# Routing on un-normalised tokens, a first gather for expert 0, the rest loop ahead of the last expert, and a diagonal norm

## The chip, the core and the metric

The kernel runs on one core of a Trainium2 chip. The metric is the device time of one launch in microseconds; less is better. The core has a matrix engine (TensorE, PE in the profile, with its weight loads as PEld), VectorE (DVE), ScalarE (ACT), GpSimd (POOL) and SyncE (SP), whose queue issues nearly all transfers, and 16 DMA engines which carry them out.

## What is computed

Two transformer blocks on 256 tokens of 1024 features. The part that matters, cut from the reference:

```python
mix = merged @ w_out[l] + b_out[l]
x = layer_norm(DEEPNORM_ALPHA * x + mix, ln1_g[l], ln1_b[l])
ffn = hier_moe(x, ...)      # 8 groups of 8 experts
x = layer_norm(DEEPNORM_ALPHA * x + ffn, ln2_g[l], ln2_b[l])

def hier_moe(...):
    _, g_sel = lax.top_k(g_logits, 1)              # one group of 8
    e_logits = jnp.take_along_axis(e_all, g_sel[:, :, None], axis=1)[:, 0]
    top_v, top_i = lax.top_k(e_logits, TOP_K)      # two experts of its 8
    weights = g_w * jax.nn.softmax(top_v, axis=-1)
    ...                                            # hdn = silu(xb @ w1[e]) * (xb @ w3[e]); hdn @ w2[e]
```

Block 2 begins with an RMS norm (`mix_norm`) ahead of its input projections (a linear recurrence and an attention), has a second one ahead of the FFN and a third ahead of the last gate.

## The kernel before

Tokens lie in two tiles t of 128 (`x1`, 128 partitions x 2 x 1024). A weight of a projection comes as a 1 MB load of 128x2048 floats; ScalarE casts it to a high half (`hlh`, L293), VectorE takes the rest as a low half (`hll`, L295), and three matmuls of the halves make up for one in full precision (L323, L324, L326 with features on partitions; L342, L343, L346 with tokens on partitions). `pump` runs small deferred pieces between the groups of a projection.

**Into the expert loop.** The out-projection (`proj_tok` in `block1`) writes the sum for LN1. `route` then normalises on VectorE (L371, L378), transposes (L785), computes 72 router logits per token (L789, L793), finds the best group and twice the best expert with `first_max` (L814 to L818), and counts with matmuls the rank of each token within its expert (L849 to L853). From the ranks, 0/1 matrices G (L971) are made for four experts at a time, and `gather` multiplies the tokens with G (L885), so that each expert gets 32 slots of features (`xg`). Softmax and slot weights (L857 to L866, L974) lie between these steps.

**The expert loop.** 64 experts of six 1 MB loads each: four for the first stage (L904), two for the halves c=0 and c=1 of the second (L921). Loads go out on SP in the order of the code, each into a buffer of a pool; the list `turn` says which pool comes next (`s1`, `g8`, `ring`, `ring2`, `ring3`, `pa`). A load waits on SP until its buffer's last reader is done, and all loads behind it wait too; eight DMA semaphores used in turn allow eight loads in flight. After a group of four experts `combine` adds its slots to the sums (L933); that of experts 56 to 59 is held back and put between the pieces of expert 63.

**Out of the loop.** 32 slots per expert may be too few; `moe_rest` loops over what is left, under a condition that every engine reads from memory (L1055) and branches on (L1056). For these inputs the loop isn't run. It stands between the two halves of expert 63's second stage. LN2 follows (L360 to L378), then block 2's first norm: squares (L1117), a factor per token (L1126, L1127), the product with the gain (L1132), 16 transposes (L1136) and the split into halves (L300).

**Ahead of the gates.** `ple_norm` does the FFN's norm and the last gate's: first eight matmuls of the gate's own projection (L1169), then the norm of both token tiles.

## Time and profile before

| | before |
|---|---|
| median of 3 runs | 1716.72 us (1716.57 to 1718.79) |
| profiled execution | 1719.65 us, span 1717.8 us |
| TensorE busy | 1486.6 us, 87% of the span |
| VectorE, ScalarE busy | 742.0 us (43%), 512.7 us (30%) |
| transfers | 537.88 MB, 313 GB/s over the span |
| first stages of the experts (L904) | 312.9 us busy, 95.1 us idle before them |

The span falls into three parts: projections of block 1 (to 267 us) with routing behind them, the expert loop (to about 1210 us), and block 2. A window row gives, for a stretch, how long each engine was busy and what the transfers moved; a timeline row gives the start and the length of a run of like instructions, and in brackets how long the engine had been idle and what released it. Matmuls overlap, so the length of a row is a little longer than the time to the next row.

### The profile page before, as it was taken

To read this page: it belongs to the slowest core of one execution; us is meant where nothing else is said; L and a number is where in the kernel's file an instruction comes from. 1 tells how busy PE (TensorE), PEld (TensorE's weight loads), DVE (VectorE), ACT (ScalarE), POOL (GpSimd) and SP (SyncE) were. 2 spreads that over 40 slices of the span, in tenths; PEclk is the share of its full clock that TensorE was granted. 3 is DMA by queue.
4 is the path that set the end of the run, shared out by engine and by line. 5 is a ranking of instruction groups with operands and counts; after the bars stand their busy time and mean duration, and the time that the engine had idled before them with its cause. 6 is when DMAs were issued, how large, how long until landed. Compare 5 with 4: busy or idle time off the path is not lost. (4 is left out here: it accounts for less than half of the span.)

```text
span 1717.8 us, 33678 instructions
## 1 busy us (share of the span) xinstructions
PE 1486.6 (87%) x14724; PEld 1158.9 (67%) x14724; DVE 742.0 (43%) x1464; ACT 512.7 (30%) x911; POOL 17.0 (1%) x22
## 2 busy tenths in 40 slices
PE   8999998867677787878878878767699999999998
PEld 7898996544344455555545545533599998899986
DVE  7999966211111111111111111111676976666645
ACT  4554542111011011011011101111395554555433
POOL 0000000000000000000000000000001000000000
PEclk9999999987777788787688878887899999999999
DMA  7565588999999999999999999999544444545552
GB/s 277 202 208 200 199 338 342 419 419 420 420 421 419 419 420 419 421 419 420 420 420 419 419 421 419 420 398 390 194 154 172 151 170 145 198 180 183 185 190 74
DMA packets 75659, 537.88 MB, mean 313 GB/s; under 512 B 8436, under 2 KB 8564, under 8 KB 11382
## 3 DMA queue, kind: packets, MB, share of 16 engines
q1 hardware_dynamic: 75506, 535.69, 78.2%
q8 instruction: 117, 1.92, 0.4%
q14 instruction: 32, 0.26, 0.0%
q10 hardware_dynamic: 4, 0.01, 0.0%
HBM read 534.62 MB, written 1.05 MB: 312 GB/s over the span
## 5 line engine op out<-in xcount | busy, mean ns | idle before, releaser
L904 PE MATMUL ps<-w,xg 128*32 128x256 f32 x4096 | 312.9, 453 | 95.1 <-DMA w<-in_wm_dram 93.9
L295 DVE TENSOR_TENSOR hll<-w,hlh 128x2048 fp32r<-128x2048 f32 (+1 forms) x114 | 257.1, 2257 | 102.6 <-PE ps L326 54.2
L904 PEld LDWEIGHTS ps<-w,xg 128*32 128x32 f32 x4096 | 135.4, 125 | 245.3 <-DMA w<-in_wm_dram 134.6
L293 ACT CAST hlh<-w 128x2048 fp32r<-128x2048 f32 (+1 forms) x114 | 214.4, 1880 | 171.2 <-PE ps L324 78.7
L323 PE MATMUL ps<-s,hlh 128*128 128x256 f32 x864 | 217.1, 289 | 0.0
L921 PE MATMUL ps<-w,hT 128*32 128x128 f32 x4096 | 177.1, 337 | 45.8 <-DVE hT L915 16.9
L324 PE MATMUL ps<-s,hlh 128*128 128x256 f32 x864 | 212.7, 284 | 0.5 <-DVE s L300 0.5
L910 DVE TENSOR_TENSOR h<-h,ps 64x256 f32<-64x256 f32 x64 | 27.1, 423 | 408.8 <-ACT h L909 408.8
L921 PEld LDWEIGHTS ps<-w,hT 128*32 128x32 f32 x4096 | 145.6, 136 | 65.3 <-issue 28.9
L323 PEld LDWEIGHTS ps<-s,hlh 128*128 128x128 f32 x864 | 165.6, 192 | 3.4 <-issue 2.2
L324 PEld LDWEIGHTS ps<-s,hlh 128*128 128x128 f32 x864 | 165.9, 192 | 1.6 <-DVE s L300 1.2
L909 ACT ACTIVATE h<-ps 64x256 f32<-64x256 f32 x64 | 24.2, 378 | 431.1 <-PE ps L904 431.1
L925 DVE COPY ys<-ps 32x128 f32<-32x128 f32 x240 | 68.2, 284 | 151.6 <-PE ps L921 149.9
L925 ACT COPY ys<-ps 32x128 f32<-32x128 f32 x240 | 62.0, 258 | 230.5 <-PE ps L921 229.1
L326 PE MATMUL ps<-s,hll 128*128 128x256 f32 x864 | 121.4, 283 | 0.0
L326 PEld LDWEIGHTS ps<-s,hll 128*128 128x128 f32 x864 | 111.5, 192 | 0.0
L505 DVE SCALAR_TENSOR_TENSOR w<-w,vec,w 128x255 f32<-128x255 f32 (+14 forms) x240 | 94.3, 465 | 0.0
L323 PE MATMUL ps<-w,hlh 128*128 128x256 f32 x352 | 86.7, 285 | 0.0
L324 PE MATMUL ps<-w,hlh 128*128 128x256 f32 x352 | 85.4, 281 | 0.0
L1109 PEld LDWEIGHTS ps<-rel,con 32*128 32x128 f32 x512 | 78.4, 236 | 10.2 <-issue 7.7
L1109 PE MATMUL ps<-rel,con 32*128 32x8 f32 x512 | 81.8, 290 | 0.0
L913 PEld LDWEIGHTS ps<-con,h 64*128 64x128 f32 x128 | 14.6, 158 | 98.8 <-DVE h L910 98.8
(342 smaller groups left out, 1774.5 us busy)
## 6 DMA issues: line engine op xcount, KB each, us to landing
w<-in_wm_dram SPq DMA_DIRECT2D x384, 1024.0 KB, 19.8
w<-in_w_dram SPq DMA_DIRECT2D x115, 1024.0 KB, 4.9
gain<-in_row_dram SPq DMA_DIRECT2D x4, 512.0 KB, 5.6
w<-in_row_dram SPq DMA_DIRECT2D x3, 512.0 KB
w<-in_wpp_dram SPq DMA_DIRECT2D x2, 768.0 KB
w<-in_xT_dram SPq DMA_DIRECT2D x2, 512.0 KB, 5.4
w<-in_w_dram SPq DMA_DIRECT2D x2, 512.0 KB, 7.3
x<-in_x_dram SPq DMA_DIRECT2D x1, 1024.0 KB, 6.7
```

The costliest lines, as they stand in the source:

```text
L293: nc.scalar.copy(hi[:, ks], src[:, ks])
L295: nc.vector.tensor_tensor(lo[:, ks], src[:, ks], hi[:, ks].bitcast(F32), ALU.subtract)
L323: nc.tensor.matmul(o, hi[:, k, ms], xh[:, k, :], start=(k == 0), stop=False)
L324: nc.tensor.matmul(o, hi[:, k, ms], xl[:, k, :], start=False, stop=False)
L326: nc.tensor.matmul(o, lo[:, k, ms], xh[:, k, :], start=False, stop=(k == 7))
L505: nc.vector.scalar_tensor_tensor(a, u[:, m, :T - d], wj, a, ALU.mult, ALU.add)
L904: r = nc.tensor.matmul(pa[j * 32:(j + 1) * 32, :256], xg[:, k, c0:c0 + CAP], w[:, j * 256:(j + 1) * 256], start=(k == 0), stop=(k == KC - ...
L909: nc.scalar.activation(h, pa[0:64, :256], AF.Silu)
L910: nc.vector.tensor_tensor(h, h, pa[64:128, :256], ALU.mult)
L921: r = nc.tensor.matmul(py[j % 2][j * 32:(j + 1) * 32, :P], hT[:, k % 2, k // 2, :], w[:, j * P:(j + 1) * P], start=(k == 0), stop=(k == 3) ...
L925: eng(ys[r0:r0 + CAP, c * 512 + j * P:c * 512 + (j + 1) * P], py[j % 2][j * 32:(j + 1) * 32, :P])
L1109: nc.tensor.matmul(ps[:, i * 8:(i + 1) * 8], self.con[0:32, o + x:o + x + P], rel, start=True, stop=True)
```

## The change

**Routing.** LN1's row loads and its VectorE passes go. The router weights are multiplied by LN1's gain (`rscale`) and centred over the features (`rcenter`, eight matmuls with ones), so the logits are computed on the un-normalised sum. The first half of its features is transposed and multiplied inside the out-projection (`xT`, `logits`); only the second half stays behind it. LN1 itself is one ScalarE operation per tile, without gain and bias, which the evacuation of the gather applies.

```diff
-            self.fg += [rbias0, nop, rbias1]
+            self.fg += [rbias0, rscale, rbias1, rcenter, nop, lambda: xT(0, 0), lambda: xT(0, 1), lambda: (logits(0, 0), logits(0, 1))]
...
+            for t in range(NT):
+                logits(1, t)
+            for t in range(NT):
+                nc.scalar.activation(x1[:, t, :], x1[:, t, :], AF.Identity, bias=nb[t], scale=rs[t])
```

The order on TensorE shows it at the end of the out-projection. Before (`ps_2592`, `ps_2621` are transposes of the two tiles, `ps_2604` logits):

```order
L346 MATMUL ps_2502<-hll_2536,m_2156 128x512 x4
L785 MATMUL ps_2592<-con,x_71 128x128 x4
L785 MATMUL ps_2598<-con,x_71 128x128 x4
L789 MATMUL ps_2604<-wsm_89,w_2582 128x72 x8
L785 MATMUL ps_2621<-con,x_71 128x128 x4
L785 MATMUL ps_2627<-con,x_71 128x128 x4
L789 MATMUL ps_2633<-wsm_89,w_2582 128x72 x4
```

Here nothing of the routing lies ahead of the last projection matmul. After, from the second of the two groups of transposes that now lie in the projection:

```order
L733 MATMUL ps_2553<-con,x_71 128x128 x4
L360 MATMUL ps_2509<-hlh_2549,m_2156 128x512
L361 MATMUL ps_2509<-hlh_2549,m_2157 128x512
L360 MATMUL ps_2509<-hlh_2549,m_2156 128x512
L361 MATMUL ps_2509<-hlh_2549,m_2157 128x512
L360 MATMUL ps_2509<-hlh_2549,m_2156 128x512
L361 MATMUL ps_2509<-hlh_2549,m_2157 128x512
L360 MATMUL ps_2509<-hlh_2549,m_2156 128x512
L361 MATMUL ps_2509<-hlh_2549,m_2157 128x512
L364 MATMUL ps_2509<-hll_2550,m_2156 128x512 x4
L740 MATMUL ps_2571<-wsm_89,w_2416 128x72 x4
L740 MATMUL ps_2576<-wsm_89,w_2416 128x72 x4
```

Behind this comes the projection's last group of 12 matmuls; the centring (L721, eight matmuls) lies some 60 instructions earlier.

**Top two, ranks, weights.** `nc.vector.max` and `match_replace` take the place of the second and third `first_max`; the ranks come from float32r matmuls on the 0/1 matrices, counted from 1; softmax and slot weights are computed after expert 0's gather.

```diff
-        v1, e1 = first_max(el, "a")
-        nc.vector.scalar_tensor_tensor(el, e1, -3.0e38, el, ALU.mult, ALU.add)
-        v2, e2 = first_max(el, "b")
+        for t in range(NT):
+            nc.vector.max(v8[:, t, :], el[:, t, :])
+        nc.vector.tensor_copy(m8[:, :, 0:2], v8[:, :, 0:2])
+        for t in range(NT):
+            nc.vector.match_replace(ee[:, t, :], m8[:, t, :], el[:, t, :], -3.3e38)
+        nc.vector.tensor_scalar(ee, ee, -3.3e38, None, ALU.is_equal)
...
-        nc.vector.tensor_scalar(rk, rk, -1.0, None, ALU.add)
```

**Gather and residual.** Expert 0's 32 slots are gathered first, between its own first matmuls; the other three experts' 96 slots after expert 0. The residual, formerly four matmuls in the routing (L802), is added at expert 4 from LN1's rows, which take a buffer of `s1` after expert 3.

```diff
+                pre = self.gather(G, xg, 1) if n0 else ()
...
+                    if e == 0:
+                        for f in self.gather(G, xg, 4, 1):
+                            f()
+                        cnt = weights()
+                        slot_weights()
...
+                    if e == 3:
+                        ln1 = self.t(self.s1, [P, 2048], "w")
+                        ln1_rows = self.spread_row(ln1[:, 0:D], "ln1_g") + self.spread_row(ln1[:, D:], "ln1_b")
+                    if e == 4:
+                        for f in ln1_rows + self.residual(ln1):
+                            f()
...
-                + [self.s1] * 2 + [self.ring] * N_RING[0] + [ring3] * N_RING[2]
+                + [self.s1] + [self.ring] * N_RING[0] + [ring3] * N_RING[2] + [self.s1]
```

Experts 60 to 63 get a list of pools of their own (`last`). On SP's queue the loads from the projection's end on stood so (a wait on `PE_49` is one for a TensorE instruction; `w_2958` is the load that waits for the projection's last matmul):

```order
L264 DMA w_2958<-in_wm_dram 128x2048 [waits DMAHW7_49,PE_49]
L264 DMA w_2960<-in_wm_dram 128x2048 [waits DMAHW0_49]
L264 DMA w_2841<-in_wm_dram 128x2048 [waits DMAHW1_49,DVE_49]
L264 DMA w_3047<-in_wm_dram 128x2048 [waits DMAHW2_49]
L264 DMA w_3049<-in_wm_dram 128x2048 [waits DMAHW3_49]
L264 DMA w_3051<-in_wm_dram 128x2048 [waits DMAHW4_49,PE_49,Activation_49]
L264 DMA w_3053<-in_wm_dram 128x2048 [waits DMAHW5_49,PE_49]
L264 DMA w_3055<-in_wm_dram 128x2048 [waits DMAHW6_49,PE_49]
L264 DMA w_3057<-in_wm_dram 128x2048 [waits DMAHW7_49,PE_49]
L264 DMA w_3193<-in_wm_dram 128x2048 [waits DMAHW0_49,PE_49]
L264 DMA w_3195<-in_wm_dram 128x2048 [waits DMAHW1_49,PE_49]
L264 DMA w_3197<-in_wm_dram 128x2048 [waits DMAHW2_49,PE_49]
```

The third needs the end of the norm, the sixth the logits, the seventh expert 0's first weight. Now (`w_2986` waits for the projection's last matmul; `w_3226` is expert 4's first weight, and its wait is for the last matmul on `w_2869`, the first half of expert 1's second stage):

```order
L264 DMA w_2986<-in_wm_dram 128x2048 [waits DMAHW4_49,PE_49]
L264 DMA w_2988<-in_wm_dram 128x2048 [waits DMAHW5_49]
L264 DMA w_2990<-in_wm_dram 128x2048 [waits DMAHW6_49]
L264 DMA w_3077<-in_wm_dram 128x2048 [waits DMAHW7_49]
L264 DMA w_3079<-in_wm_dram 128x2048 [waits DMAHW0_49]
L264 DMA w_3081<-in_wm_dram 128x2048 [waits DMAHW1_49,PE_49,Activation_49]
L264 DMA w_3083<-in_wm_dram 128x2048 [waits DMAHW2_49,PE_49]
L264 DMA w_3085<-in_wm_dram 128x2048 [waits DMAHW3_49,PE_49]
L264 DMA w_3087<-in_wm_dram 128x2048 [waits DMAHW4_49,PE_49]
L264 DMA w_3228<-in_wm_dram 128x2048 [waits DMAHW7_49,PE_49]
L264 DMA w_3226<-in_wm_dram 128x2048 [waits DMAHW0_49,PE_49]
L264 DMA w_3230<-in_wm_dram 128x2048 [waits DMAHW1_49]
```

The loads after the projection keep their number, but the waits on TensorE are spread otherwise: before, from the sixth load on every load has one; now ten loads stand ahead of `w_3226`, and behind it one without.

**Rest loop.** It moves from between the halves of expert 63's second stage to a place behind the issue of expert 63's loads and ahead of its first matmul.

```diff
                         fill, comb = self.combine(*late), self.combine(WT, ys)
-
-                        def rest():
-                            for f in comb[0:2]:
-                                f()
-                            self.moe_rest(tabs, rk, wt, s, q)
-
-                    r = self.expert(wts, xg, i * CAP, ys, i * CAP, q, fill, rest)
+                        rest = comb[0]
+                        self.moe_rest(tabs, rk, wt, s, q)
+                    r = self.expert(wts, xg, i * CAP, ys, i * CAP, q, fill, rest, pre if e == 0 else ())
```

On TensorE the branch stood before behind the first half and its two combination matmuls (`w_9951` is that half's weight):

```order
L921 MATMUL ps_10001<-w_9951,hT_9998 32x128
L933 MATMUL ps_2648<-w_9635 128x512
L933 MATMUL ps_2650<-w_9635 128x512
L1055 TENSOR_LOAD ntot_2946
L1056 COMPARE_AND_BRANCH
L1057 COMPARE_AND_BRANCH
L1057 UNCONDITIONAL_BRANCH x2
```

Now it stands behind expert 62's last matmul (on `w_9897`):

```order
L975 MATMUL ps_9975<-w_9897,hT_9950 32x128
L1135 TENSOR_LOAD ntot_2976
L1136 COMPARE_AND_BRANCH
L1137 COMPARE_AND_BRANCH
L1137 UNCONDITIONAL_BRANCH x2
```

and behind the loop, which isn't run, comes the whole of expert 63 (`w_9996` is its first weight):

```order
L1136 UNCONDITIONAL_BRANCH
L958 MATMUL ps_10214<-w_9996,xg_9650 32x256 x8
L987 MATMUL ps_2655<-ys_9213,WT_9212 128x512
L958 MATMUL ps_10214<-w_9998,xg_9650 32x256 x8
L987 MATMUL ps_2657<-ys_9213,WT_9212 128x512
L958 MATMUL ps_10214<-w_10000,xg_9650 32x256 x8
L987 MATMUL ps_2656<-ys_9213,WT_9212 128x512
L958 MATMUL ps_10214<-w_10002,xg_9650 32x256 x8
L987 MATMUL ps_2658<-ys_9213,WT_9212 128x512
L967 MATMUL ps_10254<-con,h_10251 128x64 x2
```

**First norm of block 2.** Instead of the product with the gain and transposes, each 128x128 piece of `x1` is multiplied by a diagonal matrix of the factors, which transposes and scales at once; the gain, now one value per partition, is applied at the evacuation.

```diff
+        for t in range(NT):
+            for k in range(KC):
+                nc.tensor.matmul(pss[k // 2][:, k % 2, t * P:(t + 1) * P], self.x1[:, t, k * P:(k + 1) * P], dgs[t], start=True, stop=True)
+        for k in range(KC):
+            ps, g = pss[k // 2][:, k % 2, :], self.v(name, k)
+            r = (nc.scalar.activation(hi[:, k, :], ps, AF.Copy, scale=g),
+                 nc.vector.scalar_tensor_tensor(lo[:, k, :], ps, g, hi[:, k, :].bitcast(F32), ALU.mult, ALU.subtract))
```

**Gate norms.** At the end of block 2's out-projection and of the FFN the next weight is split into halves before the norm (`split_ahead`), and `ple_norm` does tile 0's norm, the eight matmuls, tile 1's norm.

```diff
+                self.rms_T(ss, qp, hi, lo, 0)
+                pss = self.ple(c)
+                self.rms_T(ss, qp, hi, lo, 1)
```

## Rows read from the trace of the kernel before

**Rows 1.** Windows over all engines: stretch, its us, busy us by engine, granted clock, DMA.
```profile
264.00:268.60 4.60, 4.58 (x25) 3.33 (x23) 3.96 (x9) 1.06 (x3) 0.98 (x1) 1.00 0.35 121
...
268.60:290.00 21.40, 17.55 (x156) 12.57 (x155) 16.95 (x76) 6.35 (x13) 0.98 (x1) 1.00 0.84 326
...
290.00:1140.00 850.00, 666.72 (x8754) 429.62 (x8754) 146.11 (x503) 102.96 (x364) 0.00 (x0) 0.80 1.01 420
...
1208.00:1212.00 4.00, 1.02 (x3) 0.19 (x1) 0.20 (x1) 0.00 (x0) 0.00 (x0) 1.00 0.02 4
```

**Rows 2.** Waits of SP's queue, 255 to 320 us: total, times, longest, all in us.
```profile
SPq L264 <- PE ps L904: 13.9, 8, 10.7
...
SPq L264 <- DVE x L378: 5.5, 1, 5.5
```

**Rows 3.** TensorE timeline, 264 to 286 us: start, us, engine, line, operation, tiles.
```profile
266.13 1.07 PE L346 MATMUL ps<-hll,m 128*128 128x512 f32 x4
...
267.08 1.32 PE L785 MATMUL ps<-con,x 128*128 128x128 f32 x8
...
268.42 2.00 PE L789 MATMUL ps<-wsm,w 128*128 128x72 f32 x16
...
281.56 3.81 PE L885 MATMUL ps<-G,x 128*128 128x128 f32 x32 [0.85 <-DVE G L971]
```

**Rows 4.** VectorE and ScalarE timelines of the same stretch.
```profile
267.61 0.68 DVE L680 SCALAR_TENSOR_TENSOR x<-ps,x 128x512 f32<-128x512 f32 x1
...
274.44 0.29 DVE L793 SCALAR_TENSOR_TENSOR ys<-ps,brs,b_rt 128x72 f32<-128x72 f32 x1 [0.81 <-PE ps L789]
...
267.78 1.25 ACT L786 COPY w<-ps 128x512 f32<-128x512 f32 x2 [0.23 <-PE ps L785]
```

**Rows 5.** TensorE timeline, 285 to 308 us: experts 0 and 1.
```profile
285.51 3.66 PE L904 MATMUL ps<-w,xg 128*32 128x256 f32 x64
...
292.94 3.66 PE L904 MATMUL ps<-w,xg 128*32 128x256 f32 x64
...
298.32 1.95 PE L921 MATMUL ps<-w,hT 128*32 128x128 f32 x64 [0.43 <-issue]
```

**Rows 6.** The rest-loop branch, line 1056, by engine: duration in ns, start.
```profile
L1056 DVEq COMPARE_BRANCH  x1: 72/72/72, 1207.1 to 1207.1; - x1
...
L1056 PEldq COMPARE_BRANCH  x1: 3877/3877/3877, 1207.8 to 1207.8; - x1
```

**Rows 7.** TensorE timeline, 1191 to 1219 us: expert 62's end, expert 63, the branch.
```profile
1191.89 1.93 PE L921 MATMUL ps<-w,hT 128*32 128x128 f32 x32 [1.40 <-SPq L1056]
...
1194.39 1.93 PE L904 MATMUL ps<-w,xg 128*32 128x256 f32 x16 [0.57 <-SPq L1056]
...
1205.21 1.08 PE L921 MATMUL ps<-w,hT 128*32 128x128 f32 x32 [0.43 <-issue]
...
1207.07 1.96 PE L933 MATMUL ps<-w 128*128 128x512 f32 x4 [0.77 <-DVE w L925]
...
1212.13 2.05 PE L921 MATMUL ps<-w,hT 128*32 128x128 f32 x32 [3.10 <-PEq L1056]
...
1214.95 3.75 PE L933 MATMUL ps<-w 128*128 128x512 f32 x4 [0.77 <-DVE w L925]
```

**Rows 8.** TensorE and VectorE timelines, 1218 to 1232 us: block 2's first norm.
```profile
1226.75 3.91 PE L1136 MATMUL ps<-con,q 128*128 128x128 f32 x16 [8.05 <-DVE rms L1126]
...
1218.74 0.70 DVE L360 BATCH_NORM_STATS2 bst<-ps 128x6 f32<-128x512 f32 x1 [0.76 <-PE ps L933]
...
1231.32 0.69 DVE L300 TENSOR_TENSOR s<-ps,s 128x512 fp32r<-128x512 f32 x1 [0.16 <-ACT s L300]
```

**Rows 9.** TensorE timeline at the gate norms; in brackets idle time and its end.
```profile
1477.71 1.38 PE L1136 MATMUL ps<-con,q 128*128 128x128 f32 x8 [1.18 <-DVE q L1132]
...
1480.17 0.39 PE L324 MATMUL ps<-s,hlh 128*128 128x256 f32 x1 [0.51 <-DVE s L300]
...
1689.15 1.38 PE L1136 MATMUL ps<-con,q 128*128 128x128 f32 x8 [1.22 <-DVE q L1132]
```

More of the change, by code (lines that the diff above doesn't have):

```diff
@@ new lines, in route, with residual, part @@
+        return weights
+    def residual(self, ln):
+        nc = self.nc
+        g, b = ln[:, 0:D], ln[:, D:2 * D]
+        def part(t):
+            nc.vector.scalar_tensor_tensor(self.gain, self.x1[:, t, :], ALPHA, g, ALU.mult, ALU.mult)
+            nc.vector.scalar_tensor_tensor(self.gain, b, ALPHA, self.gain, ALU.mult, ALU.add)
+            for c in range(2):
+                nc.tensor.matmul(self.acc[t][c], self.c("ident"), self.gain[:, c * 512:(c + 1) * 512], start=False, stop=True,
+                                 skip_group_check=True)
+        return [lambda t=t: part(t) for t in range(NT)]
@@ L883, in gather, with part @@
+    def gather(self, G, xg, ne, e0=0):
+        nc = self.nc
+        cs, n = slice(e0 * CAP, ne * CAP), (ne - e0) * CAP
+        def part(k):
             ps = self.ps()
             for t in range(NT):
[L885 to L889 removed]
+                nc.tensor.matmul(ps[:, :n], self.x1[:, t, k * P:(k + 1) * P], G[:, t, cs], start=(t == 0), stop=(t == NT - 1))
+            if k % 2:
+                nc.scalar.activation(xg[:, k, cs], ps[:, :n], AF.Identity, bias=self.v("ln1_b", k), scale=self.v("ln1_g", k))
+            else:
+                nc.vector.tensor_scalar(xg[:, k, cs], ps[:, :n], self.v("ln1_g", k), self.v("ln1_b", k), ALU.mult, ALU.add)
+        return [lambda k=k: part(k) for k in range(KC)]
@@ L892, in expert @@
+    def expert(self, wts, xg, c0, ys, r0, q, fill=None, rest=None, pre=()):
         nc = self.nc
```

352 lines of the change are left out of this document (193 added, 159 removed).

## The prediction

> **What bounds the kernel now.** I read the page's slices first, which show a long middle part with full transfers and a TensorE that is often idle, and on either side the reverse; then the windows of these parts, then the waits and the single instructions at the seams between them. In the middle, the expert loop, the windows show 420 GB/s from 290 to 1140 us while TensorE is busy 667 of 850 us [rows 1]: the transfer of weights is the bound. At that rate a 1 MB load takes 2.50 us and an expert (six loads) 15.0 us, against 7.4 us of compute per expert when the data is there (285.51 to 292.94 [rows 5]). Before and after the loop TensorE is the bound. Three seams are thus worth money: from the projections into the loop, out of the loop, and the two norms ahead of the gate. At a seam I ask when the stream of loads runs dry and when it starts again, not how long the routing is. All sums are made against the profiled execution: 1719.65 us, with a span of 1717.8; the median of the three runs shown is 1716.72, and I move it by the same difference. 0.2% is 3.4 us, about what a measurement of this kernel can tell from no change.
>
> **Seam 1a, the projection gets longer: +4.8 us.** SP's first load after the out-projection waits for the projection's last matmul (from 266.13, done at 267.2 [rows 3]), and so it does in the new order. TensorE is busy without a gap there, so what is put ahead of that matmul delays the stream one for one. Put ahead are: eight matmuls for the centring of the router weights, which should take between a transpose's 0.165 us (eight in 1.32) and a logit matmul's 0.25 (eight, two records each, in 2.00), thus 1.3 to 2.0 us; eight transposes, 1.3 us; eight logit matmuls at 0.23 to 0.25, thus 1.8 to 2.0 [rows 3]. The sum is 4.4 to 5.3; I take 4.8. The projection ends at 272.0 and the stream, dry since about 264 and back at 268.6 before [rows 1], comes back at 273.4. The 1 MB of norm rows that goes away only lets the stream run dry earlier.
>
> **Seam 1b, the old holes go: -4.8 us.** From 268.6 to 290 the stream moved 326 GB/s, not 420: 21.4 x (1 - 326/420) = 4.8 us lost [rows 1]. Two waits of SP stand behind it: on the end of the norm (5.5 us) and on expert 0's first use of a weight (10.7 us) [rows 2]. In the new order ten loads follow the projection's end without such a wait: five need nothing later than that end, one the last logits, four expert 0's stages one after the other. Ten loads are 25.0 us: the stream is full from 273.4 to 298.4.
>
> **Seam 1c, a new hole: +5.4 us.** The eleventh load, the first to wait for more, is expert 4's first weight. The residual's rows take an s1 buffer after expert 3, so this load now waits for the s1 buffer that expert 1's second stage reads, and five loads whose buffers are free stand behind it in SP's queue. When does expert 1 get there? Before, the logits were complete 7.5 us after the projection (274.73) and the gather started 6.8 us later (281.56) [rows 3, 4]. Now the transposes and logits left after the projection are one residual add 0.7, four transposes 0.66, one copy 0.6, four matmuls 1.0, one add 0.3 and hand-overs [rows 3, 4]: 3.9 us. The chain of small VectorE operations loses its second maximum, the subtraction and the weights; counting what is left at 0.2 us each gives 4.9 us (4.3 to 6). The gather starts at 280.8. Expert 0's own gather is 16 matmuls; 16 of 128 columns took 3.81 us, but 72 columns took 0.25 each as well, so I take 3.8 for 32 columns (1.0 if columns set the price) [rows 3]. Then the first stage 3.66 and from its end to the next expert 3.8 [rows 5]: 292.1. The gather of the other three stands next, again 3.8 (2.9), with two transposes 0.4: expert 1 starts at 296.3, where it started at 292.94. It needs 6.35 us to the end of the first half of its second stage [rows 5]: 302.7, and the data flows 1.1 us later. The stream is empty for 303.8 - 298.4 = 5.4 us (1.7 to 6.6). The loop then has no other seam: the five loads behind it cover 12 us, and the waits after them are for earlier experts. So the loop ends 4.8 - 4.8 + 5.4 = **5.4 us later** (1.2 to 7.1). The gather of one expert first frees its weights earlier than before, but the price, 3.8 us more gather on TensorE, falls on expert 1.
>
> **Seam 2, the check of the rest loop: -4.8 us.** The branch costs VectorE 0.07 us and TensorE 3.88 us, during which it issues nothing [rows 6]. Before, it stood between the two halves of expert 63's second stage: TensorE finished the first half's combination at 1209.0, idled 3.1 us, then did the second half in 2.05 us where the first had taken 1.08, and the last combination from 1214.95 to 1218.7 [rows 7]. Moved ahead of expert 63, it lies behind expert 62's last matmul (1193.8), so expert 63 starts at 1197.0 and not 1194.39. From the start to the end of the first half is 11.9 us [rows 7], which makes 1208.9, when all weights have landed [rows 1], so TensorE and no longer the data sets the end. The second half adds 1.1, the four combination matmuls 3.9: 1213.9, against 1218.7. If the first 16 records (1.93) and the combination matmul behind them run at the quicker of the two paces seen here (1.08 against 2.05), it is 1.8 us better; if the branch takes longer, each microsecond is lost in full. Bounds 0 to -6.6. SP's loads for block 2, held until then by TensorE's branch, start earlier too, but the chain below does not wait for them.
>
> **Seam 2, the norm on a diagonal: -0.5 us.** From the last statistics (1218.74) to the first factors the chain on VectorE stays as long: the scaling by the column gain goes (four operations of 0.7), 16 transposes (3.91 us with waits [rows 8]) become 16 fp32 matmuls at 0.24, and the evacuation becomes eight pieces on each of ScalarE and VectorE at about 0.4, ending 13.8 us after the last statistics where it ended at 1232.0, 13.3 after [rows 8]. TensorE starts earlier on the first piece, the low halves of the weights come later. Bounds -2 to +1.5.
>
> **Seam 3, the two norms ahead of the gate: -2.0 us.** TensorE idled 1.18 and 0.51 us at the first and 1.22 at the second [rows 9], 2.9 together. Splitting the next weight ahead takes a whole split of a weight on VectorE out of the chain of the last token tile, and the gate's matmuls now stand between the two tiles' transposes. About a third stays. Bounds -0.5 to -2.9.
>
> **Sum.** +5.4 - 4.8 - 0.5 - 2.0 = -1.9 us: 1717.8 for the profiled execution, **1714.8** against the median. With all bounds on one side it would be 1706 or 1725.
>
> **Rivals.** *The hole stays small (1710.6).* If 32 columns cost a quarter, expert 0's gather takes 1.0 and the other three's 2.9; the eleventh load is released 3.7 us earlier, the hole is 1.7 and the sum -5.6; with the early stretch of expert 63 a little faster, -6.1. For it: the count of columns; against it: 72 columns cost what 128 did. *The branch is dear under load (1721).* Before, it ran at 1207.8 when the transfers stood at 4 GB/s [rows 1, 6]; now it runs in the middle of a full stream. 3.88 us for TensorE against 0.07 for VectorE is no price of a comparison, so something is fetched. Expert 63 has no slack in my sum, so what it takes over 3.9 us is lost; slower by 0.2% begins when it takes 9.2 us. At 10 us the sum is +4.2: 1720.9. For it: the fetch must share the transfer engines; against it: only that no row of before shows such a fetch in a full stream. [...] *The routing is no shorter (1717.4).* If the new VectorE chain takes as long as the old, the hole is 1.9 us longer and a part of the ten loads waits: -1.9 + 2.6 = +0.7.
>
> **How the numbers follow.** Forecast 0.42 (its own range 1712 to 1718, a quarter of it faster), small hole 0.28, dear branch 0.18, routing no shorter 0.12. Faster: 0.42 x 0.25 + 0.28 x 0.9 = 0.36. Slower: the dear branch and a little of the last, 0.20. Same: 0.44. The range leaves one in ten on either side: 1708 to 1722.
>
> **What would show it.** Right: the projection's last matmul near 272; GB/s full for 25 us after the restart, then some 5 us near nothing around 299 to 304, ended by expert 1's second stage; expert 63's first matmul 3 us after expert 62's last, the last combination 4.8 us earlier relative to the loop's last load; TensorE's idle at the two gate norms under 0.5 us. Wrong: no hole at 299 (first rival); a branch of TensorE well over 4 us or an idle of that length ahead of expert 63 (second); the gather at 281.5 or later (third).

## The result: 20 us slower, and the profile after

| | before | after |
|---|---|---|
| median | 1717.1 us (1716.6 to 1718.8, 4 runs) | 1737.2 us (1732.9 to 1740.7, 4 runs) |
| profiled execution | 1719.65 us, span 1717.8 | 1736.4 us, span 1734.6 |

The ratio is 1.0114, with a 95% interval of 1.0090 to 1.0138: slower by about 20 us, where 1714.8 us was forecast. The two spans differ by 16.8 us; the rest of the 20 is that the profiled execution of before lay 2.5 us above its median and that of the changed kernel 0.8 below. The sums below go by the spans.

**Into the loop.** TensorE's timeline of the changed kernel (start, us, line, tiles; in brackets the idle time ahead and what ended it):

```profile
273.03 1.11 PE L740 MATMUL ps<-wsm,w 128*128 128x72 f32 x8 [0.44 <-ACT w L734]
278.00 0.45 PE L874 MATMUL ps<-WT,W 128*128 128x128 f32 x1 [3.86 <-DVE gain L893]
...
279.25 2.77 PE L930 MATMUL ps<-G,x 128*128 128x32 f32 x12 [0.22 <-DVE G L1034]
281.95 1.08 PE L958 MATMUL ps<-w,xg 128*32 128x256 f32 x8
...
291.99 2.79 PE L958 MATMUL ps<-w,xg 128*32 128x256 f32 x24
...
299.88 3.81 PE L930 MATMUL ps<-G,x 128*128 128x96 f32 x32
...
303.84 3.66 PE L958 MATMUL ps<-w,xg 128*32 128x256 f32 x64
...
309.47 1.96 PE L975 MATMUL ps<-w,hT 128*32 128x128 f32 x64 [0.38 <-DVE hT L969]
```

The shorter chain does what it says: the logits are done at 274.1 and the gather starts at 279.25, where 280.8 was forecast. But TensorE has nothing to do in the chain (3.86 us idle; in the old order the residual's matmuls stood there), and then everything is slow: 12 gather records of 32 columns take 2.77 us, and 24 records of the first stage take 2.79, about double the time per record of expert 1, where 64 take 3.66. The gather and the first stage of expert 0 last from 279.25 to 294.8, 15.5 us; the forecast had 3.8 and 3.66 for the two. The windows of the same kernel (stretch, its us, busy us by engine, granted clock, DMA share, GB/s) give the reason:

```profile
275.00:285.00 10.00, 6.78 (x37) 4.93 (x37) 5.39 (x37) 1.87 (x5) 0.00 (x0) 0.53 1.01 428
285.00:295.00 10.00, 9.78 (x68) 5.29 (x64) 0.62 (x2) 2.19 (x4) 0.00 (x0) 0.50 0.83 298
295.00:300.00 5.00, 3.89 (x67) 3.28 (x68) 1.28 (x4) 0.74 (x3) 0.00 (x0) 0.55 0.53 198
300.00:312.00 12.00, 10.37 (x180) 8.12 (x184) 7.93 (x32) 3.87 (x12) 0.00 (x0) 1.00 0.28 94
...
255.00:285.00 30.00, 25.13 (x141) 20.37 (x139) 13.76 (x56) 7.51 (x13) 1.08 (x2) 0.84 0.75 301
285.00:325.00 40.00, 34.26 (x542) 23.99 (x542) 12.62 (x47) 8.75 (x25) 0.00 (x0) 0.82 0.67 258
```

The granted clock is 0.50 from 276, within the idle stretch, until 299.5; before, it was 1.00 from 264 to 290 [rows 1] and on to 325 (rows below). TensorE's last logit ended at 274.1, and in the window from 275.5 to 276 the clock is 0.65: it fell within the idle 3.86 us, and the work behind them began at 0.50.

And the stream of weights stops, from 302.9 to 311.4. The waits of SP's queue, 285 to 312 us (total, times, longest):

```profile
SPq L264 <- PE ps L958: 17.7, 3, 10.5
SPq L264 <- PE ps L975: 16.7, 2, 11.6
```

The 11.6 us are the load that the prediction named, expert 4's first, behind expert 1's second stage. To compare kernels I count the transfer lost in a stretch as its length times (1 - rate/420). The kernel before:

```profile
255.00:285.00 30.00, 26.96 (x151) 21.02 (x150) 20.09 (x67) 5.16 (x11) 1.96 (x2) 1.00 0.87 350
285.00:325.00 40.00, 34.22 (x628) 23.22 (x630) 13.79 (x53) 8.95 (x28) 0.00 (x0) 1.00 0.95 388
```

Lost up to 285: 5.0 us before, 8.5 after. From 285 to 325: 3.0 before, 15.4 after. Together 15.9 us more, and at the last half of expert 62's second stage the loop is 15.0 us late (1206.87 below, against 1191.89 [rows 7]).

**Out of the loop.** TensorE's timeline and, below it, the branch of line 1136 (ns, start):

```profile
1206.87 1.08 PE L975 MATMUL ps<-w,hT 128*32 128x128 f32 x32 [1.21 <-SPq L1136]
1214.27 1.93 PE L958 MATMUL ps<-w,xg 128*32 128x256 f32 x16 [6.32 <-PEq L1136]
...
1228.45 2.94 PE L987 MATMUL ps<-w 128*128 128x512 f32 x6
...
1236.93 6.06 PE L1233 MATMUL ps<-con,x 128*128 128x128 f32 x32 [5.53 <-DVE con L1209]
1243.19 0.38 PE L341 MATMUL ps<-s,hlh 128*128 128x256 f32 x1 [0.20 <-ACT s L1236]
...
1273.52 0.58 PE L360 MATMUL ps<-hlh,s 128*128 128x512 f32 x1
```

```profile
L1136 PEldq COMPARE_BRANCH  x1: 6146/6146/6146, 1207.8 to 1207.8; - x1
```

The branch takes 6.15 us, not 3.88, and TensorE idles 6.32 us ahead of expert 63. From expert 62's last half (1206.87) to the end of the last combination (1231.4) are 24.5 us, before 26.8 [rows 7]: a gain of 2.3. The norm: from the last combination to the first projection matmul 11.8 us in both, but its 32 records take 6.06 us, and to the first token-major projection matmul it is 42.1 us, before 40.3 (1218.7 to this row of before):

```profile
1258.99 0.58 PE L342 MATMUL ps<-hlh,s 128*128 128x512 f32 x1
```

**Gate norms.** TensorE at both, then VectorE at the first:

```profile
1487.30 1.38 PE L1223 MATMUL ps<-con,q 128*128 128x128 f32 x8 [0.55 <-DVE q L1219]
1488.52 3.60 PE L1268 MATMUL ps<-w 128*128 128x512 f32 x8
1493.57 1.38 PE L1223 MATMUL ps<-con,q 128*128 128x128 f32 x8 [1.45 <-DVE q L1219]
...
1699.61 1.32 PE L1223 MATMUL ps<-con,q 128*128 128x128 f32 x8 [0.54 <-DVE q L1219]
...
1705.87 1.38 PE L1223 MATMUL ps<-con,q 128*128 128x128 f32 x8 [1.50 <-DVE q L1219]
```

```profile
1488.43 2.28 DVE L295 TENSOR_TENSOR hll<-w,hlh 128x2048 fp32r<-128x2048 f32 x1
1490.63 1.28 DVE L316 TENSOR_TENSOR s<-ps,s 128x512 fp32r<-128x512 f32 x2
1491.83 0.20 DVE L1202 TENSOR_SCALAR rms<-rss 128x1 f32<-128x1 f32 x1
```

TensorE now idles 4.0 us at the two norms (0.55, 1.45, 0.54, 1.50), before 2.9 [rows 9]. The gate's eight matmuls wait behind tile 0's transposes, and tile 1's factor (L1202) behind the split of a weight (L295) and behind tile 0's low halves (L316). From the first token-major matmul of block 2 to TensorE's last the kernel takes 455.5 us, before 453.4: 2.1 us longer.

The four places together: +15.0 - 2.3 + 1.8 + 2.1 = +16.6 us, against 16.8 between the spans.

### The profile page after: what moved, and what is told of

Its sections match the earlier page's. It is cut to its first block, busy times and chain, and to the rows that moved or that the text cites. A ratio compares the mean times of both kernels' runs of the same rounds, so it can differ in the third digit from the quotient of the medians.

```text
span 1734.6 us, 33807 instructions
## 1 busy us (share of the span) xinstructions
PE 1502.6 (87%) x14790; PEld 1162.5 (67%) x14790; DVE 750.0 (43%) x1469; ACT 530.0 (31%) x926; POOL 15.7 (1%) x22
## 5 line engine op out<-in xcount | busy, mean ns | idle before, releaser
L958 PE MATMUL ps<-w,xg 128*32 128x256 f32 x4096 | 323.0, 459 | 99.0 <-DMA w<-in_wm_dram 92.1
L295 DVE TENSOR_TENSOR hll<-w,hlh 128x2048 fp32r<-128x2048 f32 (+1 forms) x112 | 252.5, 2256 | 96.0 <-PE ps L344 53.7
L293 ACT CAST hlh<-w 128x2048 fp32r<-128x2048 f32 (+1 forms) x112 | 210.4, 1880 | 163.4 <-PE ps L342 78.1
L975 PE MATMUL ps<-w,hT 128*32 128x128 f32 x4096 | 181.0, 343 | 41.5 <-DVE hT L969 18.6
L1190 PEld LDWEIGHTS ps<-rel,con 32*128 32x128 f32 x512 | 74.1, 224 | 9.7 <-issue 7.5
L1190 PE MATMUL ps<-rel,con 32*128 32x8 f32 x512 | 77.5, 282 | 0.0
```

Of the source, the lines that this page charges most:

```text
L293: nc.scalar.copy(hi[:, ks], src[:, ks])
L295: nc.vector.tensor_tensor(lo[:, ks], src[:, ks], hi[:, ks].bitcast(F32), ALU.subtract)
L958: r = nc.tensor.matmul(pa[j * 32:(j + 1) * 32, :256], xg[:, k, c0:c0 + CAP], w[:, j * 256:(j + 1) * 256], start=(k == 0), stop=(k == KC - ...
L975: r = nc.tensor.matmul(py[j % 2][j * 32:(j + 1) * 32, :P], hT[:, k % 2, k // 2, :], w[:, j * P:(j + 1) * P], start=(k == 0), stop=(k == 3) ...
L1190: nc.tensor.matmul(ps[:, i * 8:(i + 1) * 8], self.con[0:32, o + x:o + x + P], rel, start=True, stop=True)
```

## The experiments

The first theory was **A, the clock**: the fall to half speed is the loss. Its rivals were **B, the order** (the gather in two pieces), and **C, the place in the queue** (the residual's tile takes a buffer, so that one load waits long and holds those behind it). Ratios are to the kernel before, run on the same chip beside each. The letters stand for other theories where an expectation says so.

### e1: fillers for TensorE in the chain

```diff
+        for i in range(20):
+            nc.tensor.matmul(self.acc[i % 2][i // 2 % 2][:, 0:144], ident, lg.rearrange("p t e -> p (t e)"), start=True, stop=True)
```

> The changed kernel with one addition: 20 matmuls of the identity with the logits (128x144, results overwritten before they are used) stand on TensorE between the logits and the ranks, where the changed kernel leaves it idle for 3.86 us. They add work and no result. Theory A (the clock): the loss comes from the granted clock of 0.50 between 276 and 299 us, in which the gather and the first stage of expert 0 take twice their time. Then the clock here stays at 1.00, expert 0's first stage ends near 285 instead of 294.8, expert 1 starts near 292 instead of 303.8, SyncE's 11.6 us wait for expert 1 is nearly gone, and the time falls by 10 to 13 us to 1724 to 1727. Theory B (the order): the gather in two pieces and the place of the residual's tile in the load queue hold the stream, whatever the clock. Then expert 1 starts after 300 also here, the hole before 311 stays over 6 us, and the time is 1734 or more.

1733.0 us, ratio 1.0090 (1.0068 to 1.0111). The fillers took 5.17 us, a little more than the chain's gap, and put the gather off to 280.57. From 285 to 325 us the clock was 1.00, where the changed kernel had 0.82, and expert 1 started 6.9 us earlier than there. Windows and TensorE's timeline:

```profile
285.00:325.00 40.00, 34.03 (x575) 24.18 (x576) 14.47 (x52) 10.55 (x30) 0.00 (x0) 1.00 0.81 332
```

```profile
296.90 3.66 PE L960 MATMUL ps<-w,xg 128*32 128x256 f32 x64
```

The loss in this stretch falls from 15.4 to 8.4 us, by 7.0. The time falls by some 4 us, not by 10 to 13: expert 62's last matmul ends 7.1 us earlier (1200.85 against 1207.95), but from there to the end of the last combination this run needs 26.0 us and the changed kernel 23.4, so that 2.6 of the 7.1 are gone again. The hole did not go: SP still waited 11.1 us for expert 1's second stage. So the clock is part of the loss and not all of it. Both theories had the start of expert 1 wrong and the time too, B by 1 us; B was right on the hole.

### e2: the same idle time in the kernel before

```diff
-        acc0(0)
...
-        acc0(1)
```

> The kernel before, with its eight residual matmuls between logits and ranks left out, so that the residual is missing from the sum (the first combination starts the accumulators). Order, gather and queues are those of before; TensorE now idles some 5 us ahead of the ranks, more than the 3.86 us of the changed kernel. Theory A (the clock): the granted clock falls to 0.50 ahead of the ranks, the gather takes some 7.5 us instead of 3.81 and expert 0's first stage some 7 instead of 3.66, and the kernel gets slower by 6 to 10 us, 1723 to 1727, although it does less work. Theory B (the order): the clock is beside the point here, the time stays within 1 us of the kernel before.

1719.6 us, ratio 1.0006 (0.9995 to 1.0018): no change in time, as B said. The trace tells more. After the idle 5.51 us the clock stood at 0.50, and the gather took 6.29 us instead of 3.81; the stretch from 285 lost 6.2 us of transfer instead of 3.0 (row below), and expert 62's last half started 5.4 us later than before (1197.31). Yet the last combination ended only 1.2 us later. The branch behind the loop took 0.37 us instead of 3.88: TensorE waited 0.41 us there instead of 3.10, and the clock stayed at 1.00 where it had been 0.50 before, so that the second half and the combinations behind it were 2.4 us shorter; a new stop of 1.16 us within that half took a part back. Timeline, windows and branch (line 1054 here):

```profile
283.14 6.29 PE L883 MATMUL ps<-G,x 128*128 128x128 f32 x32 [0.60 <-DVE G L969]
```

```profile
285.00:325.00 40.00, 34.22 (x582) 25.53 (x582) 13.23 (x50) 8.95 (x29) 0.00 (x0) 0.96 0.88 355
```

```profile
1216.28 1.06 PE L919 MATMUL ps<-w,hT 128*32 128x128 f32 x26 [1.16 <-issue]
1217.95 1.98 PE L931 MATMUL ps<-w 128*128 128x512 f32 x4 [0.61 <-ACT w L923]
```

```profile
L1054 PEldq COMPARE_BRANCH  x1: 369/369/369, 1212.9 to 1212.9; - x1
```

An unchanged time was here, in the profiled execution, the sum of two effects. e11 and e12 take up the branch.

### e3: one gather of four experts, as before

```diff
-                n0 = 0 if g else 1
+                n0 = 0
...
-                pre = self.gather(G, xg, 1) if n0 else ()
+                for f in self.gather(G, xg, 4):
+                    f()
```

> The changed kernel, but all four experts of the first group are gathered at once ahead of expert 0, as before (no separate gather of expert 0); the combine weights still come behind expert 0. Theory A (the clock): the clock is still 0.50; the gather takes about 7.6 us from 279.3, expert 0's first stage ends near 294.5 as in the changed kernel (294.8), expert 1 starts right behind expert 0 near 300 instead of 303.8, and the hole before expert 1's release is 3 to 4 us shorter: 1732 to 1735. Theory B (the order): without the second gather between experts 0 and 1 the stream is as in the kernel before, and the time falls by 10 us or more, to 1727 or less.

1728.4 us, ratio 1.0065 (1.0043 to 1.0086): 9 us of the 20 are gone, more than A and less than B allowed. Timeline and windows:

```profile
278.47 5.88 PE L930 MATMUL ps<-G,x 128*128 128x128 f32 x32 [0.29 <-DVE G L1037]
284.28 3.66 PE L958 MATMUL ps<-w,xg 128*32 128x256 f32 x64
...
291.87 3.66 PE L958 MATMUL ps<-w,xg 128*32 128x256 f32 x64
```

```profile
280.00:285.00 5.00, 5.00 (x43) 4.62 (x46) 1.86 (x6) 1.97 (x5) 0.00 (x0) 0.72 1.00 421
285.00:325.00 40.00, 33.97 (x620) 23.07 (x612) 13.44 (x50) 9.61 (x28) 0.00 (x0) 1.00 0.87 351
```

The clock fell here too, after the same idle 3.85 us, but it was back before 285, within the gather; in the changed kernel it stayed at 0.50 until 299.5, although TensorE was nearly as busy (9.78 of 10 us from 285 to 295). Expert 1 starts at 291.9, 12 us earlier: 4 of that are the second gather, which no longer stands between experts 0 and 1, and nearly all of the rest is the clock. The loss from 285 on is 6.6 us; SP still waits 10.9 us for expert 1's second stage.

### e4: the rest loop back in its old place

```diff
-                        rest = comb[0]
-                        self.moe_rest(tabs, rk, wt, s, q)
+                        def rest():
+                            comb[0]()
+                            self.moe_rest(tabs, rk, wt, s, q)
```

> The changed kernel with the rest loop put back between the two second-stage halves of expert 63. From the end of expert 62 to the end of the last combination the kernel before took 24.9 us and the changed one 23.4, although its branch took 6.15 us instead of 3.88. Theory A: the move is worth this 1.4 us, so undoing it costs 1 to 2 us (1738 to 1740), and the branch takes about 3.9 us again because no weights are loading then. Theory B: the move is worth the 4.8 us that the prediction gave it, and something else after the loop took the rest: undoing it costs 4 to 5 us (1741 to 1742). Theory C: the longer branch eats the whole gain: undoing it changes less than 0.7 us.

Here one combination matmul stands ahead of the branch; in the kernel before it was two. 1739.2 us, ratio 1.0119 (1.0100 to 1.0138); by time not to be told from the changed kernel. By trace, expert 62's last half to the end of the last combination is 25.9 us (1208.28 to 1234.15) against 24.5, and the branch takes 3.37 us, with 4 GB/s of transfers under way. That is A: the move is worth 1.4 us.

### e5: the residual's tile after expert 4's loads

```diff
                     wts = [load(wm[e, j]) for j in range(6)]
+                    if e == 4:
+                        ln1 = self.t(self.s1, [P, 2048], "w")
...
-                    if e == 3:
-                        ln1 = self.t(self.s1, [P, 2048], "w")
```

> The changed kernel with one move: the tile of the residual's gain and bias rows is taken from the pool s1 after the six loads of expert 4 instead of ahead of them, so that expert 4's first load gets a buffer that expert 0's first stage frees, not one that expert 1's second stage frees. Theory C (the place in the queue): the waiting load held every load behind it on SyncE, and that is most of the loss. Then SyncE's 11.6 us wait for the second stage (PE, source of the second expert matmul) before 311 us is gone, the stretch 285 to 315 loses under 6 us of transfer instead of 15.5, and the time falls by 8 to 11 us, to 1726 to 1729. Theory A (the clock): the half clock alone delays every release; the stretch still loses 10 us or more and the time stays at 1732 or above.

1733.4 us, ratio 1.0093 (1.0080 to 1.0106): 4 us, half of what C said, and a time that A allowed. The long wait for the second stage is gone (2.4 us at most are left of it), and from 285 to 315 the loss is 4.4 us, as C said. But SP then waited 7.2 us for the transfer of the residual's rows, whose buffer now waits for that stage, and 4.9 us more were lost from 315 to 325. SP's wait, 285 to 325 us, and the window:

```profile
SPq L264 <- DMA w<-in_row_dram: 7.2, 1, 7.2
```

```profile
285.00:325.00 40.00, 34.27 (x563) 23.45 (x557) 13.46 (x50) 9.53 (x28) 0.00 (x0) 0.87 0.85 323
```

9.2 us are lost instead of 15.4. A part of this is the clock, which here was low from 278 to 295 and not from 276 to 299.5; expert 1 starts 1.1 us earlier.

### e6 and e7: the remedies together

e6 is e3 with ten fillers as in e1; e7 adds e5's move.

> The run with all four experts gathered at once (1728.4), with ten filler matmuls of the identity with the logits added between logits and ranks as in the run with twenty. Theory A (the clock): the clock stays at 1.00, the gather takes 3.8 instead of 5.9 us and expert 1 starts near 289.5 instead of 291.9: 2 to 3 us faster than without the fillers, 1725 to 1727; the rest of the hole stays because of the place in the queue. If the clock were all of it, the hole would vanish and the time be near 1721.

> All three together: four experts gathered at once, ten fillers for the clock, the residual's tile taken after expert 4's loads. If clock, order of the gather and place in the queue are the whole loss of the loop's start, the stretch 285 to 315 loses under 3 us of transfer, as in the kernel before, and the time is 1720 to 1723; the 3 to 5 us that are left against the kernel before lie in the later restart of the stream (272 against 268.6 us) and in block 2. If something else holds the loop, the time stays above 1725.

e6: 1727.0 us, 1.0064 (1.0051 to 1.0076). The time is in A's range, but not for A's reason: in the profiled execution the clock still fell (0.72 from 280 to 285) and the gather took 5.44 us, so this is e3 again. e7: 1725.5 us, 1.0050 (1.0036 to 1.0063). The time lies just above the 1725 from which something else was to hold the loop. But in its profiled execution the same fillers held the clock at 1.00, and the hole is gone. The window of e7, then two of e14, a run further down with the same start of the loop in which the fillers did not hold the clock (0.70, gather 5.44 us):

```profile
285.00:325.00 40.00, 33.51 (x606) 22.24 (x598) 13.86 (x51) 8.80 (x28) 0.00 (x0) 1.00 1.01 415
```

```profile
280.00:285.00 5.00, 5.00 (x41) 4.56 (x43) 1.72 (x5) 2.11 (x5) 0.00 (x0) 0.70 1.01 423
285.00:325.00 40.00, 33.83 (x616) 22.44 (x608) 13.61 (x51) 9.46 (x28) 0.00 (x0) 1.00 1.00 411
```

e7 loses 0.5 us and e14 0.9, less than before (3.0). No single remedy does it (with the clock held 8.4 us were left, with one gather 6.6, with the tile moved 9.2). One gather and the moved tile together are enough, although the clock falls for a while in e14; whether the clock and one of the two would do was not run. The last combination of e7 ends at 1218.9, as before (1218.7), and still the span is 5.8 us longer: +1.8 to the first token-major projection, +3.6 from there to the end (2.1 of it as in the changed kernel, in e1 and in e3 to e6, 1.5 in this execution alone).

### e8 and e9: the norms undone

e8 is e7 with `ple_norm` in its old order and without `split_ahead`; e9 is e8 with the old first norm (gain, transposes).

> The run before this one, with the third seam undone: at the two gate norms both tokens' factors are computed first and the norm's transposes follow the gate's matmuls, as in the kernel before, and no weights are split ahead at the last projection halves. By the trace of the changed kernel the first vector pass of token half 0 now stands ahead of token half 1's factor, and the two norms together took 2.1 us longer than before: undoing this gives 1.5 to 2.5 us, 1718 to 1721. By the prediction's step (the new order saves 2.0 us) undoing it would cost 2 us.

> The run with the old gate norms (1722.5), with the first norm of block 2 undone too: a factor times gain pass on VectorE, sixteen transposes, the gain row loaded at expert 8. What stays of the second seam's second half is the rule that the first splits of block 2 are issued behind the norm. Theory A: the diagonal norm itself costs the 1.8 us by which the stretch from the last combination to the first token-major projection grew (40.3 to 42.1 us): its 32 products take 6 us where 16 transposes took 3.9, and VectorE's eight passes keep the first weights' splits back. Then the stretch is 40.3 again and the time 1720 to 1721. Theory B: the issue rule of the splits costs it; then the stretch stays at 42 and the time at 1722 to 1723.

e8: 1722.5 us, 1.0030 (1.0019 to 1.0041), 3.0 below e7 but above the 1718 to 1721 that were expected. The stretch from the first token-major matmul to the end takes 453.5 us, before 453.4, in the changed kernel 455.5. The new gate order and the split ahead together cost the 2.1 us; the prediction's step had the wrong sign. e9: 1724.3 us, 1.0024 (1.0014 to 1.0034): by time not to be told from e8, and outside what both theories gave; by trace 40.8 us from the last combination to the first token-major matmul instead of 42.1, so 1.4 of the 1.8 us are the diagonal norm. e7 and e8 are the same up to block 2, and yet their last combinations end 3.0 us apart: so much do single executions of the loop differ, and for less the trace of one stretch is the better measure.

### e10: the rest loop in the middle of the expert loop

```diff
-                            self.moe_rest(tabs, rk, wt, s, q)
...
+                    if e == 32:
+                        self.moe_rest(tabs, rk, wt, s, q)
```

> The kernel before with one move: the rest loop stands behind expert 32's matmuls, in the middle of the expert loop, where TensorE idles between experts, instead of between the second-stage halves of expert 63. Theory A: the branch costs TensorE 4 to 6 us there, which its idle time covers, and the 3.1 us of waiting at expert 63 are gone with the interrupted chain behind it: 3 to 5 us faster, 1712 to 1714. Theory B: SyncE and the transfers have to pass the branch too, the stream of weights dries up for a few us at expert 32, and since the stream sets the loop's pace this gives back what the end gains: 1716 to 1719, with a dip in the transfer rate near 750 us.

1722.2 us, 1.0020 (1.0011 to 1.0029): slower, more than B said. SyncE reaches the branch at 720.1 us and issues its next load at 746.55, right behind TensorE's branch (742.8 to 746.4), and the stream dries up: 13.1 us of transfer are lost between 700 and 800 us. The end gains: from expert 62's last matmul to the last combination 18.8 us instead of 24.9. Two windows (last the clock, DMA share and GB/s):

```profile
735.00:740.00 5.00, 4.32 (x71) 2.47 (x69) 1.39 (x6) 1.02 (x3) 0.00 (x0) 1.00 0.32 129
740.00:745.00 5.00, 2.29 (x66) 1.88 (x66) 1.64 (x6) 1.03 (x4) 0.00 (x0) 1.00 0.02 5
```

### e11 and e12: the branch moved in the instruction stream

The edit of e11 to the kernel before; e12 has 123 in the place of 60. The small matmuls (128x16, their results unused) stand behind experts 10 to 12, where TensorE idles, and only move TensorE's later instructions: by 239 places on in e11, by 491 in e12. By theory P the place of the branch in this stream sets what the branch costs, and both kernels should take 1714 to 1716 us.

```diff
+                    if 10 <= e < 13:
+                        ps = self.ps()
+                        for i in range(60 // 3):
+                            nc.tensor.matmul(ps[:, :16], self.c("ident"), iota[:, 0:16], start=True, stop=True)
```

> [...] Leaving out eight matmul passes moved them by 17 places the other way, and there the branch over the rest loop took 0.37 us instead of 3.88. [...] Theory L (one lucky execution, or the changed timing of that run): the branch takes 3.4 to 4 us and the time is that of before within 1 us.

> [...] Theory L: 3.4 to 4 us, and the time of before within 1 us. [...]

e11: 1717.6 us, 0.9994 (0.9985 to 1.0003). e12: 1716.7 us, 0.9989 (0.9981 to 0.9998), the only kernel here that is faster than the kernel before clear of noise, by a tenth of a per cent; both lie above the 1714 to 1716 of theory P. TensorE's timeline of e11, then of e12, with e63's second half behind the branch:

```profile
1209.50 0.54 PE L921 MATMUL ps<-w,hT 128*32 128x128 f32 x6 [0.41 <-PEq L1060]
1211.39 1.06 PE L921 MATMUL ps<-w,hT 128*32 128x128 f32 x26 [1.35 <-issue]
```

```profile
1209.25 0.54 PE L921 MATMUL ps<-w,hT 128*32 128x128 f32 x8 [0.41 <-PEq L1060]
```

On the branch theory P holds: it takes 0.46 us in both, and the wait falls from 3.10 to 0.41. TensorE then stops for 1.35 us after 6 records, in e12 after 8. The code of e12 stands 252 places behind that of e11 (491 against 239); why the branch is short at these places, and why TensorE stops where it does, no run shows.

### e13 to e15: place or traffic

e13 is the changed kernel, e14 is e9, and e15 is the kernel before with the rest loop moved as the change does it, each with small matmuls behind expert 10 (26, 31 and 51) meant to bring the branch to the place it has in e12. What the traces show of that place is the stop behind the branch: it comes after 7, 9 and 8 records, in e12 after 8.

> [...] Theory P (place): the branch takes under 1.5 us instead of 6.1 although weights are loading, the wait ahead of expert 63 falls from 6.3 to under 2 us, and the time falls by 3 to 5 us to 1732 to 1734. Theory T (traffic): the branch waits for code behind the weights of the last expert and still takes 5 to 6 us; the time stays at 1736 to 1738.

> The run with all but the shorter chain and the moved rest loop mended or undone (1724.3, branch 6.0 us), padded to the same place. Theory P: branch under 1.5 us, 3 to 5 us faster: 1719 to 1721. What is then left against the kernel before, 1 to 3 us, is the later restart of the stream. Theory T: 1723 to 1725.

> The kernel before with the rest loop moved ahead of the last expert as the change does it (with its buffer lists for the last four experts), padded to the same place. If the move is worth what the prediction gave it (4.8 us) once the branch is short: 1711 to 1713. If the weights of the last expert are late there anyway and the chain behind them sets the end: within 1 us of the two padded runs of the kernel before (1716.7 and 1717.6).

e13: 1740.1 us, 1.0126 (1.0112 to 1.0141). e14: 1725.7 us, 1.0043 (1.0029 to 1.0057). e15: 1721.1 us, 1.0017 (1.0007 to 1.0027). None got faster; e13 and e14 lie just above the range of theory T, e15 above both of its expectations. The profiled execution of e13 is its longest, 1748.4 us. The timeline of e13, and of e15:

```profile
1218.68 1.07 PE L958 MATMUL ps<-w,xg 128*32 128x256 f32 x7 [4.90 <-PEq L1140]
1224.11 1.44 PE L958 MATMUL ps<-w,xg 128*32 128x256 f32 x9 [4.35 <-issue]
```

```profile
1195.37 1.08 PE L904 MATMUL ps<-w,xg 128*32 128x256 f32 x8 [3.74 <-PEq L1066]
1200.73 1.08 PE L904 MATMUL ps<-w,xg 128*32 128x256 f32 x8 [4.28 <-issue]
```

The padding that made the branch short in a quiet stretch goes with two waits in a full one: 4.9 and 4.35 us, 3.74 and 4.28, in e14 2.2 and 3.9. The branch itself takes 4.7, 2.7 and 3.5 us (e13 to e15), where it took 0.46 in e11 and e12. That points to the traffic: the stop of 1.35 us in e11 and e12 began when nothing moved (0 GB/s in a half microsecond just ahead of it), those of about 4 us in e13 to e15 with 200 to 300 GB/s under way. It is not settled, since the mean rates over the stops overlap (205 and 126 GB/s against 318, 210 and 220). In e15 the move is a loss: its time is 4 us above the two padded kernels with the loop in its old place.

## Why the prediction was wrong

**Seam 1a**, +4.8: the dry stretch lost 8.5 us of transfer, before 3.3 up to 268.6 (4.6 us at 121 GB/s [rows 1]), so +5.2. The size was right by luck: the projection ended at 270.3 and not at 272.0, but ahead of that end the stream lost some 2 us more than before, as it ran dry earlier, which the sum had at nothing.

**Seams 1b and 1c**, -4.8 and +5.4: this step failed. The hole was where it was said to be, and its end was the one named, expert 1's second stage; but it was sized with durations of before, at a granted clock of 1.00, for a TensorE that the same change leaves idle ahead of them. Expert 0's gather and first stage were put at 3.8 and 3.66 us; they took 15.5, and 8.6 with the clock held (e1). With the clock held, expert 1 starts at 296.9, where 296.3 was forecast, and the hole loses 8.4 us instead of 5.4: the stream came back earlier than forecast, so the ten loads were through at 297 and not at 298.4, and it flowed again at 305 to 306, not at 303.8. At half clock expert 1 starts at 303.8, and the first weights of expert 0 are freed late as well, so that the stream is thin from 287 on; the loss is 15.4 us. The losses of seam 1 add up to 5.2 - 4.8 + 15.4 = 15.8 us instead of 5.4: 7.0 more by e1 for the clock, 3.0 for a hole that is longer with the clock held as well, 0.4 at the restart.

The prediction priced the idle chain at its length alone. The residual matmuls, which the change moves to expert 4, had been what kept the clock up: e2, which only leaves them out, shows the fall in the kernel before as well (0.96 from 285 to 325 us where it had been 1.00, the gather 6.29 us instead of 3.81).

**Seam 2, the rest loop**, -4.8: measured -2.3 from expert 62's last half, and -1.4 from its last matmul, the mark of the sum (23.4 us to the last combination, before 24.9). The gap to -4.8 is the idle time ahead of expert 63, 6.32 us where the sum had 3.1, with a branch of 6.15 us instead of 3.88. The rival that names the traffic had this mechanism, at a smaller size than the 9.2 us at which it was to decide; the runs fit it (3.4 to 3.9 us in quiet stretches, 4.1 to 6.2 in the stream) and do not settle it. Of the fetch that it supposes the traces show one packet of 0.02 MB on the instruction queue while TensorE's branch lasts, between 1208.8 and 1209.0 us before and between 1211.4 and 1211.6 after; that the branch waits for it no view says.

**Seam 2, the diagonal norm**, -0.5: measured +1.8, just outside its bounds. Its own working did not give its sign: an evacuation that ends 13.8 us after the last statistics, before 13.3, is later by half a microsecond. The evacuation ended 16.6 us after them (1248.0 against 1231.4). The 16 matmuls at 0.24 us, 3.8 together, came as 32 records in 6.06 us: after 5.5 us without work TensorE had a granted clock of 0.50 up to 1240 and 0.73 from there to 1243. The 16 transposes of before, 3.91 us, had 0.50 too, but they were half as many records. And ScalarE's last piece waited behind the cast of a whole weight (1.94 us). The low halves of the next weights then came late, as the prediction said of them without a price: TensorE waited 0.63 and 0.40 us for them.

**Seam 3**, -2.0: measured +2.1, the wrong sign. The step counted the split as taken out of the chain of the last tile. By VectorE's rows a split of a weight, the next one, still stands ahead of tile 1's factor, tile 0's low halves have joined it there, and the gate's matmuls, which had covered the norm's start, now wait for tile 0.

**Rivals.** The hole did not stay small; the routing is as short as forecast (the gather starts 1.5 us earlier than in the sum, as the projection ends 1.7 earlier). No rival had the clock. But without the clock's loss too the range of 1708 to 1722 would have been missed: e1, with the clock held, takes 1733.0. The rest is the longer hole, the branch, and the two norms with the wrong sign.

Open stays where the remaining 4 us of e9 come from. Its trace says in which part they lie: expert 62's last matmul ends 5.9 us later than before (1199.7 against 1193.8), and from there to the end the kernel is within 0.3 us of before. Transfers lost up to 325 us make 1.1 of this (9.1 us against 8.0). Another 1.7 us, by estimate, are the pace of the loop: from 400 to 1100 us each window of 100 us moves 420 GB/s in the kernel before, and in e2, e11, e12 and e15, which are built on it; in the changed kernel and every run built on it (e1, e3 to e9, e13, e14) it is 418 or 419, and 1 GB/s in 700 us is 1.7 us. No run says why. Single executions differ by as much as what is left.

## What to carry to other kernels

Where a change removes matmuls from a stretch in which TensorE waits, do not take durations over from before without the granted clock they were measured at: work that seemed off the path may be what holds the clock (here the residual matmuls: without them the gather took 6.29 us and not 3.81, e2). When a load queue is served in order, follow each buffer's last reader after every new tile in its pool; one tile more can put a late wait ahead of loads that are free (here for 11.6 us). And put a branch that all engines pass where transfers are few, and not into the stream (in e10 that lost 13.1 us of transfer).

## What the runs showed of the hardware

- The granted clock stayed at 0.50 from 276 to 299.5 us in the changed kernel, most of it with a busy TensorE (9.78 of 10 us between 285 and 295) at work on the gather of 32 columns and the expert stage. In e5, with the same instructions there, it was low from 278 to 295. In e3, where a gather of 128 columns followed the same idle time, it was back before 285.
- Ten fillers held the clock in the profiled executions of e7, e8 and e9 and did not in those of e6 and e14, with the same instructions at that place. TensorE's idle time behind them was 0.75 us.
- A wait of TensorE cost more than its length: behind the branch of the kernel before (3.10 us of waiting) the clock was 0.50, and the last half and the combinations took 6.57 us; in e2 (0.41 us) it stayed at 1.00, and they took 4.2 us, the stop of 1.16 not counted.
- One and the same branch took TensorE 0.37 to 6.24 us: 0.37 to 0.46 with few transfers and the code moved by 17 places back, 239 on and 491 on (e2, e11, e12), 3.4 to 3.9 at other places with few transfers (before, e4, e10), 4.1 to 6.24 with weights loading (after, e1, e3, e5 to e9); 2.7 to 4.7 with weights loading and the code moved so that a second stop, of 3.9 to 4.35, comes after 7 to 9 records (e13 to e15).
